# Token mixers of a hybrid block broken into parts and ordered by estimated ends of operations

## The chip, the cores and the metric

The kernel runs on one core of a Trainium2 chip. The metric is device time in microseconds (us). A profiled execution shows five engines: TensorE (PE; its weight loads are PEld), VectorE (DVE), ScalarE (ACT), GpSimd (POOL) and SyncE (SP), which starts most DMAs. An instruction stands in the queue of its engine and starts when the semaphores that it waits for have come.

## What is computed

Two layers of a hybrid backbone, batch 1, with 256 latent and 256 context tokens of width 1024. Four mixers read one input projection; their outputs are projected, gated and summed:

```
def token_mixers(hx, hc, p, rope_ret, rope_mla, need_ctx_out):
    (conv_x, z_x, xbc_x, dt_x, rq_x, rk_x, rv_x, rg_x, cq_x, ckv_x, kr_x, gl_x) = split_cols(hx @ p['w_in'], IN_SPLITS)
    ...
    ssm_yx, _ = ssm_mixer(z_x, xbc_x, dt_x, p, ssm_hc, True)
    ret_yx, _ = retention_mixer(rq_x, rk_x, rv_x, rg_x, p, ret_hc, rope_ret, True)
    att_x = block_attention(mla_q(cq_x, p, rope_mla), jnp.concatenate([k_c, k_x], axis=1), ...)
    out_x = merge_branches((conv_module(conv_x, p), ssm_yx, ret_yx, att_x), gl_x, p)
def conv_module(u, p):
    a, g = jnp.split(u, 2, axis=-1)
    h = dwconv(a * jax.nn.sigmoid(g), p['conv_w'], p['conv_b'])
    return jax.nn.silu(layernorm(h, p['conv_ln_g'], p['conv_ln_b']))
def merge_branches(branches, gate_logits, p):
    merged = sum(sigmoid(gate_i) * (branches[i] @ p['w_branch'][i]))
    return merged @ p['w_out']
```

(the last function is written shorter here). The convolution has 31 taps over 512 channels. Before the mixers stands a modulated RMS norm, behind them a SwiGLU block. In layer 1, the last, only the latent tokens are read on, so most of it works on N = 256 tokens, against N = 512 in layer 0.

## The kernel before

Activations lie transposed, channels on 128 partitions and tokens along the row. A float32 product is made of three fast matmuls of rounded halves (`mm3`): high by high, high by low, low by high. Weights come in one stream of chunks of 128 x 1024; for each, SP issues a 512 KB load (`raw`), ScalarE casts it (`whi`) and VectorE makes the remainder in two subtractions of 512 columns (`wlo`); `w_ensure` (line 347) keeps them some chunks ahead. Results of TensorE go to eight banks of 512 columns, four named `mm` (projections) and four named `mx` (mixers). All other tiles (`u`) come from 70 slots of a pool `U`.

The mixing stage of a layer is written by five generators. `lin` (line 740) holds what is TensorE's: the input projection (queries, keys, gated convolution inputs and so on), the gates, and the branch projections in the order state-space (1), MLA (3), retention (2), convolution (0); for branch i it waits for the token `br{i}`, which the mixer i gives. `ssm` (932), `ret` (1123), `mla` (1214) and `conv` (1344) are the mixers. Each `yield` gives the order back to `interleave` (585), and may name a token that must be there before the generator goes on, or, with a plus sign, give one. `interleave` takes `lin` by default, and a mixer when a count of VectorE's work (`clk["dve"]`, plain sums of durations, and `mixed`) lies more than LOOK behind the count of TensorE's. The mixers run in two rows, by MIX: `chain` (1384) runs ssm, mla and ret after one another, beside it stands `conv`. `conv` waits for `br1` and `br2` before its taps.

```
MIX = ("smr c", "smr c")
            w = min(can, key=lambda w_: steps[w_] if w_ else -1)
            if len(can) > 1 and w == 0 and max(clk["dve"], mixed) + lookahead < clk["pe"]:
                w = min(can[1:], key=lambda w_: steps[w_])
```

On TensorE the order of the program is kept for the mixers: `PE._place` ties each of their matmuls behind the last one of `lin` that was written before. On the other engines a scheduler goes by priorities: mostly the order of the program, with the work inside `tc.high_priority()` (weight preparation, evacuation of projections, row scales) ahead.

In `conv` a tap is one VectorE operation over a tile (`taps`, line 728); there are four tiles, in pairs. Then the four are added, `tok_sums` (502) sums the channels on TensorE (`mx<-one,u`), the mean is spread with `bcast` (532; `mx<-cons,mean`), subtracted, the squares are added, transposed and reduced (`rstd_of`, 513; `mx<-cons,u`), a row scale is made of ten tiny operations (`rs_y`), spread (`mx<-cons,rs_y`) and applied, followed by tanh and products. `tt` and `stt` are VectorE's two-operand helpers.

## Time and profile before

| | before |
|---|---|
| median of 3 runs | 1692.0 us (1687.25 to 1694.21) |
| profiled execution, its own time | 1692.55 us |
| its span, first to last instruction | 1690.8 us |
| mean granted TensorE clock | 0.994 |
| TensorE busy | 1641.8 us, 97% |
| VectorE busy | 1312.9 us, 78% |
| ScalarE busy | 812.0 us, 48% |

The mixers of layer 0 run mainly between 100 and 400 us of the span, those of layer 1 between 1100 and 1350; the last branch projection of layer 1 ends at about 1460. Busy time is the time in which an engine has an instruction at work; the share is that of the span. The ends of matmuls are modelled, so rows of TensorE overlap, and its pace is better read from start to start.

### The profile page before, as it was taken

What the parts mean: (1) busy time and instruction counts of PE and PEld (TensorE: products, weight loads), DVE (VectorE), ACT (ScalarE), POOL (GpSimd) and SP (SyncE); (2) the same over time, 40 slices, a digit from 0 to 9 for tenths busy, and PEclk for the clock granted to TensorE, in tenths of its full rate; (3) what the DMA queues carried; (4) which work ended last, traced back from release to release, by engine and by line L of the source; (5) the groups of instructions that cost most, each with busy time, mean ns of one, the idle gap of its engine ahead of it and who ended that gap; (6) DMA issues with size and microseconds to landing.
All of it is one profiled execution on the core that took longest, in us unless ns stands there. A gap on an engine that the chain in (4) does not pass through costs nothing.

```text
span 1690.8 us, 24270 instructions
## 1 busy us (share of the span) xinstructions
PE 1641.8 (97%) x8926; PEld 1359.7 (80%) x8926; DVE 1312.9 (78%) x2676; ACT 812.0 (48%) x1378; POOL 53.5 (3%) x89
## 2 busy tenths in 40 slices
PE   6999999999999999999999999999999999999998
PEld 4777766778888888988888889978778788778887
DVE  4779999988578568887666757699889967887765
ACT  3475759462234233522212235457577545455654
POOL 0020200000000000000000000001110000000000
PEclk9999999999999999999999999999999999999999
DMA  9353321214445445465456646445433377646664
GB/s 362 122 145 113 114 68 54 75 38 131 157 126 185 130 157 187 128 196 165 148 174 190 228 146 203 143 126 164 123 100 101 100 221 244 211 152 189 185 188 141
DMA packets 85096, 259.04 MB, mean 153 GB/s; under 512 B 9648, under 2 KB 18784, under 8 KB 84976
## 3 DMA queue, kind: packets, MB, share of 16 engines
q1 hardware_dynamic: 73584, 244.15, 45.8%
q10 hardware_dynamic: 10624, 12.28, 2.9%
q0 software_dynamic: 768, 1.05, 0.3%
q8 instruction: 70, 1.15, 0.3%
q14 instruction: 50, 0.41, 0.1%
HBM read 253.70 MB, written 2.18 MB: 151 GB/s over the span
## 4 chain that ended last, share of the span: by engine, by line
PE 86%; DVE 5%; DMA 4%; ACT 3%; issue 1%; POOL 0%; ACTq 0%; DVEq 0%; SPq 0%
PE mm L187 74%; PE mx L187 9%; DMA u<-drow 3%; PE mx L191 2%; DVE u L226 2%; ACT u L163 2%; DVE wlo L230 1%; DVE u L230 1%; ACT whi L168 1%; ACT u L168 1%; DVE u L241 0%; DMA u<-u 0%; DMA u<-xin 0%; DMA raw<-w_ada 0%; DMA drow<-u 0%
## 5 line engine op out<-in xcount | busy, mean ns | idle before, releaser
L187 PE MATMUL mm<-u,whi 128*128 128x512 f32 (+1 forms) x4088 | 1149.6, 362 | 3.7 <-DVE u L226 1.8
L187 PEld LDWEIGHTS mm<-u,whi 128*128 128x128 f32 x4088 | 728.1, 189 | 130.5 <-issue 12.1
L187 PE MATMUL mm<-u,wlo 128*128 128x256 f32 (+1 forms) x2332 | 785.3, 337 | 0.0
L168 ACT CAST whi<-raw 128x1024 fp32r<-128x1024 f32 x351 | 368.4, 1050 | 548.7 <-PE mm L187 328.8
L230 DVE TENSOR_TENSOR wlo<-raw,whi 128x512 fp32r<-128x512 f32 x702 | 461.7, 688 | 165.7 <-ACT whi L168 164.4
L187 PEld LDWEIGHTS mm<-u,wlo 128*128 128x128 f32 x2332 | 441.8, 189 | 47.0 <-issue 2.0
L226 DVE SCALAR_TENSOR_TENSOR u<-raw,cs,u 128x512 f32<-128x512 f32 x210 | 148.2, 746 | 80.7 <-DMA raw<-w_ada 80.6
L163 ACT ACTIVATE u<-u 128x256 f32<-128x256 f32 (+5 forms) x262 | 122.7, 484 | 150.5 <-DVE u L230 105.8
L187 PE MATMUL mm<-whi,u 128*128 128x512 f32 x544 | 172.7, 394 | 0.5 <-ACT u L163 0.5
L230 DVE TENSOR_TENSOR u<-u,u 128x256 f32<-128x256 f32 (+5 forms) x290 | 160.3, 571 | 8.3 <-ACT u L163 3.2
L187 PE MATMUL mx<-u,u 128*64 128x256 f32 (+6 forms) x644 | 132.1, 396 | 12.3 <-ACT whi L168 3.8
L226 DVE SCALAR_TENSOR_TENSOR u<-u,convw,u 128x510 f32<-128x510 f32 (+29 forms) x240 | 134.0, 599 | 0.0
L187 PEld LDWEIGHTS mx<-u,u 128*64 128x64 f32 (+3 forms) x644 | 79.8, 165 | 54.3 <-issue 13.5
L187 PEld LDWEIGHTS mm<-whi,u 128*128 128x128 f32 x544 | 101.8, 188 | 23.3 <-issue 1.7
L187 PE MATMUL mm<-wlo,u 128*128 128x512 f32 x272 | 106.4, 391 | 0.0
L163 ACT ACTIVATE u<-mm 128x512 f32<-128x512 f32 (+3 forms) x110 | 60.6, 553 | 40.1 <-PE mm L187 35.7
L226 DVE SCALAR_TENSOR_TENSOR u<-u,mm 128x512 f32<-128x512 f32 (+1 forms) x94 | 60.0, 647 | 19.8 <-PE mm L187 18.2
L226 DVE SCALAR_TENSOR_TENSOR u<-u,u 128x256 fp32r<-128x256 f32 (+3 forms) x113 | 61.0, 550 | 10.3 <-ACT u L163 10.3
L187 PEld LDWEIGHTS mm<-wlo,u 128*128 128x128 f32 x272 | 51.1, 188 | 10.7 <-issue 0.4
L168 ACT COPY u<-mx 128x512 f32<-128x512 f32 (+4 forms) x82 | 38.5, 495 | 38.1 <-PE mx L187 36.4
L191 PE MATMUL mx<-cons,u 128*128 128x128 f32 (+1 forms) x292 | 44.1, 276 | 4.8 <-DVE u L230 3.1
L1056 POOL TENSOR_SCALAR_AFFINE_SELECT u<-u 128x256 f32<-128x256 f32 x24 | 17.4, 726 | 983.2 <-DVE u L241 825.5
(116 smaller groups left out, 890.3 us busy)
## 6 DMA issues: line engine op xcount, KB each, us to landing
raw<-wst SPq DMA_DIRECT2D x354, 512.0 KB, 3.7
raw<-w_ada SPq DMA_DIRECT2D x72, 512.0 KB, 4.1
u<-wfirst SPq DMA_DIRECT2D x32, 256.0 KB, 6.0
u<-drow ACTq DMA_DIRECT2D x32, 256.0 KB, 4.7
u<-xin SPq DMA_DIRECT2D x16, 256.0 KB, 4.3
u<-w_ada SPq DMA_DIRECT2D x16, 256.0 KB, 5.3
u<-drow ACTq DMA_DIRECT2D x16, 128.0 KB, 3.9
spill<-u SPq DMA_DIRECT2D x8, 128.0 KB, 3.6
```

The costliest lines, as they stand in the source:

```text
L163: nc.scalar.activation(o, *a, **k)
L168: nc.scalar.copy(o, i)
L187: PE._place(nc.tensor.matmul(*a, **k))
L191: PE._place(nc.tensor.transpose(*a, **k))
L226: V.scalar_tensor_tensor(out=o, in0=i0, scalar=s, in1=i1, op0=op0, op1=op1)
L230: V.tensor_tensor(out=o, in0=i0, in1=i1, op=op)
L1056: G.affine_select(out=a_[:, 0:4:3], in_=a_[:, 0:4:3], pattern=[[0, 2], [1, 128]], compare_op=ALU.is_ge, fill=-1e5, base=0, channel_multipl ...
```

## The change

The mixers are cut into units, and their work is put in order by estimated times instead of sums. `spent` gives every operation an estimated end on its engine (`Line`, a timeline with gaps) and notes when its tile is ready (`done_at`) and when its inputs are free (`free_at`). A generator may then yield `at(...)`, an "@time": go on when TensorE's estimate has reached the time at which these tiles are ready. A token "#n" waits for n free slots of `U`. `stagger` runs up to two units of a row of mixers at once, if 12 slots are free. MIX has three rows now: ssm; mla and ret after one another; and conv, which is taken last. `interleave` takes the first mixer that can go on while VectorE's estimated work lies less than LEAD ahead of TensorE, then `lin`. `ret` and `mla` have units too (`turn`, `one_head`, `end`, and `setup` for mla), and the row scales are made by `rstd_later`, which yields between steps; so does `win`, once inside a projection. `conv` no longer waits for `br1` and `br2`, but for 18 free slots ahead of each pair of tiles, and its taps get a low priority. `urgent` is `tc.high_priority` together with a mark for the estimates. DMAs that GpSimd issues are not estimated.

```diff
-MIX = ("smr c", "smr c")
-LOOK = (7e3, 3e3)
-PACE = (1.4, 1.5)
+MIX = ("s mr c", "s mr c")
+LEAD = (6e3, 5e3)
...
+class Line:
+    def __init__(self):
+        self.t, self.gaps = 0.0, []
+    def ahead(self, now):
+        return self.t - now - sum(b - max(a, now) for a, b in self.gaps if b > now)
+    def put(self, ready, dur, now=0.0):
+        self.gaps = [g for g in self.gaps if g[1] > now]
+        for i, (a, b) in enumerate(self.gaps):
+            s = max(a, ready)
+            if s + dur <= b:
+                self.gaps[i:i + 1] = [g for g in ((a, s), (s + dur, b)) if g[1] - g[0] > 50]
+                return s + dur
+        s = max(self.t, ready)
+        if s - self.t > 50:
+            self.gaps.append((self.t, s))
+        self.t = s + dur
+        return self.t
...
+    def spent(e, o, ins, dur):
+        now = clk["pe"].t
+        r = max([done_at.get(i.tensor.name, 0.0) for i in ins if hasattr(i, "tensor")], default=0.0)
+        if e == "pe":
+            end = clk["pe"].t = max(now, r if who["now"] else 0.0) + dur
+        elif who["urgent"]:
+            end = max(now, r) + dur
+            clk[e].t = max(clk[e].t, now) + dur
+        else:
+            end = clk[e].put(max(r, now), dur, now)
+        done_at[o.tensor.name] = max(done_at.get(o.tensor.name, 0.0), end + (100 if e == "pe" else 130))
+        for i in ins:
+            if hasattr(i, "tensor"):
+                free_at[i.tensor.name] = max(free_at.get(i.tensor.name, 0.0), end)
+    def at(*ts_):
+        def last_(t):
+            return max(map(last_, t), default=0.0) if isinstance(t, (tuple, list)) else done_at.get(t.tensor.name, 0.0)
+        bank = free_at.get(banks[NMM - 8], 0.0) if len(banks) >= 8 - NMM else 0.0
+        return f"@{max(last_(ts_), bank) + 200}"
...
+        r = sm([128, len(sums), N // 128], "toks")
+        for i, tiles in enumerate(sums):
+            yield at(tiles)
+            p = mx()
+            for b in range(N // 128):
+                PE.transpose(p[:, b * 128:(b + 1) * 128], tiles[0][:, b * 128:(b + 1) * 128], ident)
+            red(r[:, i, :], p[:, :N].rearrange("p (b t) -> p b t", t=128), ADD)
+        ts(r, r, 1.0 / n, MUL, EPS, ADD)
+        rs = rsqrt(r, [128, len(sums), N // 128])
+        yield at(rs)
+        return rs
...
-    def interleave(lin, others, lookahead):
+    def met(r):
+        if r is None:
+            return True
+        if r[0] == "#":
+            return len(U.free) >= int(r[1:])
+        return float(r[1:]) <= clk["pe"].t if r[0] == "@" else r in who["done"]
+    def stagger(units, wide):
+        units, live = iter(units), []
+        while True:
+            n = next((n_ for n_, (_, r) in enumerate(live) if met(r)), None)
+            if n is None and len(live) < (wide if len(U.free) >= ROOM else 1):
+                g = next(units, None)
+                if g is not None:
+                    live.append((g, None))
+                    continue
+            if n is None:
+                if not live:
+                    return
+                late = [r for _, r in live if r[0] == "@"]
+                yield min(late, key=lambda r: float(r[1:])) if late else live[0][1]
+                if late or met(live[0][1]):
+                    n = next((n_ for n_, (_, r) in enumerate(live) if met(r)), None)
+                else:
+                    continue
+            g = live[n][0]
+            try:
+                r = next(g)
+            except StopIteration:
+                del live[n]
+                continue
+            if r is not None and r[0] == "+":
+                who["done"].add(r[1:])
+                r = None
+            live[n] = (g, r)
+            if r is None:
+                yield None
...
+    def interleave(lin, others):
         gens, done = [lin, *others], set()
-        mixed = clk["dve"]
-        alive, waits, steps = set(range(len(gens))), [None] * len(gens), [0] * len(gens)
+        who["done"] = done
+        alive, waits = set(range(len(gens))), [None] * len(gens)
+        def can(w):
+            return w in alive and met(waits[w])
         while alive:
-            can = [w for w in sorted(alive) if waits[w] is None or waits[w] in done]
-            assert can, waits
-            w = min(can, key=lambda w_: steps[w_] if w_ else -1)
-            if len(can) > 1 and w == 0 and max(clk["dve"], mixed) + lookahead < clk["pe"]:
-                w = min(can[1:], key=lambda w_: steps[w_])
+            ahead, few = clk["dve"].ahead(clk["pe"].t), len(U.free) < ROOM
+            conv = len(gens) - 1
+            w = next((w_ for w_ in range(1, conv + 1) if can(w_) and (ahead < LEAD[w_ == conv] or few and w_ < conv)), None)
+            if w is None and can(0) and not (few and any((waits[w_] or "-")[0] == "@" for w_ in alive)):
+                w = 0
+            if w is None:
+                w = next((w_ for w_ in range(1, len(gens)) if can(w_) and (w_ < conv or alive <= {0, conv})), None)
+            if w is None:
+                late = [(float(waits[w_][1:]), w_) for w_ in sorted(alive) if (waits[w_] or "-")[0] == "@"]
+                assert late, waits
+                w = min(late)[1]
             waits[w] = None
-            steps[w] += 1
-            before = clk["dve"], clk["act"]
             who["now"] = w
             try:
...
+            def end():
+                yield "squares0"
+                yield "squares1"
+                rs = yield from rstd_later(accs, N, 4 * 256)
+                U.put(accs)
+                for g in range(2):
+                    yield at(rs)
+                    rb = bcast(rs[:, g, :], N)
+                    for i in (2 * g, 2 * g + 1):
+                        stt(Y[i][:, :N], Y[i][:, :N], dpar[:, 4 + i:5 + i], rb[:, :N], MUL, MUL)
+                br[1] = [Y[i] for i in range(4)]
+                yield "+br1"
+            yield setup()
             for g in range(2):
-                rb = bcast(rs[:, g, :], N)
-                for i in (2 * g, 2 * g + 1):
-                    stt(Y[i][:, :N], Y[i][:, :N], dpar[:, 4 + i:5 + i], rb[:, :N], MUL, MUL)
-            br[1] = Y
-            yield "+br1"
+                u, xt, bc, gt = {}, {}, {}, []
+                for c in (2 * g, 2 * g + 1, 4 + g, 6 + g):
+                    yield short(c, xt, u, bc)
+                yield scores(g, bc, gt)
+                for pr in (2 * g, 2 * g + 1):
+                    yield two(pr, xt, u, gt)
+                yield squares(g, gt)
+            yield end()
...
+                kt, qt = kq.pop(h)
+                yield at(kt, qt)
+                px = first(kt, qt)
+                yield at(px)
+                pts[h] = second(px)
+                yield f"+weights{h}"
...
         def conv():
-            yield "br1"
-            hs = [U([128, N]) for _ in range(4)]
-            yield "br2"
+            hs = []
             for i in (0, 2):
                 yield f"gated{i + 1}"
+                yield "#18"
+                hs += [U([128, N]) for _ in range(2)]
                 gens = [taps(hs[i + e_], R["gated", i + e_], N,
                              lambda j, o=(i + e_) * CW: convw[:, o + j:o + j + 1], CW, P("convb", i + e_))
                         for e_ in range(2)]
-                for n_, _ in enumerate(zip(*gens)):
-                    if n_ % 2:
-                        yield
+                for n_ in range(CW + 1):
+                    with tc.high_priority(offset=-600):
+                        for g_ in gens:
+                            next(g_, None)
+                    yield
                 U.put(R.pop(("gated", i)), R.pop(("gated", i + 1)))
             t = U([128, N])
             tt(t[:, :N], hs[0][:, :N], hs[1][:, :N], ADD)
             for i in (2, 3):
                 tt(t[:, :N], t[:, :N], hs[i][:, :N], ADD)
+            yield at(t)
             m = sm([128, 1, nb], "mean")
             ts(m, tok_sums([[t]], N), 1.0 / 512, MUL)
             U.put(t)
+            yield at(m)
             mb = bcast(m[:, 0, :], N)
...
-        def chain(*gens):
-            for g in gens:
-                yield from g()
         parts = {"s": ssm, "m": mla, "r": ret, "c": conv}
-        clk["dve"] = clk["pe"] if last else began
-        interleave(lin(), [chain(*(parts[x] for x in w)) for w in MIX[l].split()], LOOK[l])
+        for e in ("dve", "act", "pool"):
+            clk[e].t, clk[e].gaps = clk["pe"].t, []
+        *ones, behind = MIX[l].split()
+        interleave(lin(), [stagger(itertools.chain(*(parts[x]() for x in y)), WIDE[l]) for y in ones] + [parts[behind]()])
```

The order of the instructions, of both versions, at three places of layer 1. In the names `mm` is a bank of a projection, `u_9403` and the like are the projections' inputs or mixer tiles, `whi` and `wlo` the weights.

TensorE around the convolution's normalization, before:

```order
L187 MATMUL mm_13365<-whi_13323,u_13103 128x512
L187 MATMUL mx_13413<-one,u_13408 128x1 [waits PE_49]
L187 MATMUL mx_13413<-one,u_13408 128x1
L187 MATMUL mm_13444<-whi_13368,u_9403 128x512 [waits Activation_49]
L187 MATMUL mm_13444<-wlo_13369,u_9403 128x512 [waits DVE_49]
L187 MATMUL mm_13444<-whi_13368,u_9404 128x512
L187 MATMUL mm_13445<-whi_13368,u_9403 128x512 [waits Activation_49]
L187 MATMUL mm_13445<-wlo_13369,u_9403 128x512
L187 MATMUL mm_13445<-whi_13368,u_9404 128x512
L191 MATMUL mx_13417<-cons,mean_13412 128x128 [waits DVE_49]
L191 MATMUL mx_13417<-cons,mean_13412 128x128
L187 MATMUL mm_13444<-whi_13368,u_9405 128x512
```

and in the changed kernel (`mm_13725` belongs to branch 2, `mm_13856` is the first projection of branch 0):

```order
L220 MATMUL mm_13725<-whi_13709,u_13677 128x512
L220 MATMUL mm_13725<-wlo_13710,u_13677 128x512
L220 MATMUL mm_13725<-whi_13709,u_13677 128x512
L220 MATMUL mx_13783<-one,u_13778 128x1 [waits DVE_49,PE_49]
L220 MATMUL mx_13783<-one,u_13778 128x1
L225 MATMUL mx_13787<-cons,mean_13782 128x128 [waits DVE_49]
L225 MATMUL mx_13787<-cons,mean_13782 128x128
L225 MATMUL mx_13804<-cons,u_13791 128x128 [waits DVE_49,PE_49]
L225 MATMUL mx_13804<-cons,u_13791 128x128
L225 MATMUL mx_13821<-cons,rs_y_13809 128x128 [waits DVE_49,PE_49]
L225 MATMUL mx_13821<-cons,rs_y_13809 128x128
L220 MATMUL mm_13856<-whi_13709,u_13844 128x512 [waits Activation_49]
```

Before, projections stood between the sums, the spread of the mean and the later steps; now these steps follow one another.

VectorE at the same place, before (the sums of the four tiles, `u_13408`, stand 50 rows further up, behind the last tap):

```order
L230 TENSOR_TENSOR wlo_13388<-raw_13302,whi_13387 128x512 [waits DMAHW3_49,Activation_49]
L230 TENSOR_TENSOR wlo_13388<-raw_13302,whi_13387 128x512
L226 SCALAR_TENSOR_TENSOR u_12868<-u_12868,mm_13364 128x512 [waits PE_49]
L226 SCALAR_TENSOR_TENSOR u_12870<-u_12870,mm_13365 128x512 [waits PE_49]
L239 TENSOR_SCALAR mean_13412<-mx_13413 128x2 [waits PE_49]
L230 TENSOR_TENSOR wlo_13449<-raw_13321,whi_13448 128x512 [waits DMAHW4_49,Activation_49]
L230 TENSOR_TENSOR wlo_13449<-raw_13321,whi_13448 128x512
L230 TENSOR_TENSOR u_11522<-u_11522,mx_13417 128x256 [waits PE_49]
L230 TENSOR_TENSOR u_11522<-u_11522,mx_13417 128x256
```

and in the changed kernel (in all 14 taps stand in a row from the ninth row on, then an addition to `u_13778`, two more taps and another addition; the mean comes next):

```order
L262 SCALAR_TENSOR_TENSOR u_13009<-u_11156,convw_9888,u_13009 128x244
L262 SCALAR_TENSOR_TENSOR u_13009<-u_11156,convw_9888,u_13009 128x245
L262 SCALAR_TENSOR_TENSOR u_13210<-u_13210,mm_13724 128x512 [waits PE_49]
L266 TENSOR_TENSOR wlo_13754<-raw_13688,whi_13753 128x512 [waits DMAHW0_49,Activation_49]
L262 SCALAR_TENSOR_TENSOR u_13212<-u_13212,mm_13725 128x512 [waits PE_49]
L266 TENSOR_TENSOR wlo_13754<-raw_13688,whi_13753 128x512
L266 TENSOR_TENSOR u_12355<-u_12355,u_13210 128x512 [waits DVE_49]
L266 TENSOR_TENSOR u_12357<-u_12357,u_13212 128x512 [waits DVE_49]
L262 SCALAR_TENSOR_TENSOR u_13009<-u_11156,convw_9888,u_13009 128x244
L262 SCALAR_TENSOR_TENSOR u_13009<-u_11156,convw_9888,u_13009 128x245
```

The taps of the second pair of tiles now stand last, behind the additions for branch 2.

TensorE at the first output of the state-space mixer, before:

```order
L187 MATMUL mm_11488<-u_9404,whi_11299 128x512
L187 MATMUL mm_11488<-u_9403,wlo_11300 128x512
L187 MATMUL mm_11488<-u_9405,whi_11299 128x512
L187 MATMUL mm_11488<-u_9406,whi_11299 128x512
L187 MATMUL mx_11438<-u_11347,u_10690 64x256 [waits DVE_49,Activation_49]
L191 MATMUL mx_11456<-cons,u_10619 128x128 x2
L187 MATMUL mm_11488<-u_9405,wlo_11300 128x512
L187 MATMUL mm_11488<-u_9407,whi_11299 128x512
```

and in the changed kernel:

```order
L220 MATMUL mm_11159<-u_9403,wlo_11096 128x256 [waits DVE_49]
L220 MATMUL mm_11159<-u_9405,whi_11095 128x256
L225 MATMUL mx_10760<-cons,rs_y_10748 128x128 [waits DVE_49,PE_49]
L225 MATMUL mx_10760<-cons,rs_y_10748 128x128 x3
L220 MATMUL mx_10881<-u_10546,u_10393 64x256 [waits PE_49]
L220 MATMUL mx_10881<-u_10578,u_10393 64x256
```

The output's matmuls (`64x256`) waited for VectorE and ScalarE; now they follow the spreads of a row scale and wait for TensorE's own banks alone.

## Rows read from the trace of the kernel before

**Rows 1.** The page's part 1: engine, busy us, share of the span, instructions.

```profile
PE 1641.8 (97%) x8926; PEld 1359.7 (80%) x8926; DVE 1312.9 (78%) x2676; ACT 812.0 (48%) x1378; POOL 53.5 (3%) x89
```

**Rows 2.** Windows: busy us of PE, PEld, DVE, ACT, POOL; clock; DMA share.

```profile
100.00:400.00 300.00, 291.76 (x1397) 219.72 (x1396) 282.78 (x571) 191.53 (x386) 26.36 (x38) 0.99 0.29 86
1100.00:1350.00 250.00, 239.67 (x1368) 197.27 (x1367) 227.92 (x553) 162.82 (x319) 25.59 (x40) 0.98 0.41 119
1343.00:1462.00 119.00, 117.55 (x528) 96.48 (x526) 89.98 (x175) 60.44 (x80) 0.00 (x0) 1.00 0.73 234
1419.00:1455.00 36.00, 36.00 (x161) 29.59 (x160) 31.81 (x58) 19.47 (x27) 0.00 (x0) 1.00 0.83 276
```

**Rows 3.** The same for instructions that read the convolution's weights, VectorE alone.

```profile
62.00:412.00 350.00, 84.76 (x124) 1.00 0.31 92
1343.00:1462.00 119.00, 4.06 (x10) 1.00 0.73 234
```

**Rows 4.** What TensorE waited for, 100 to 400: us in total, times, longest.

```profile
PE mx L191 <- DVE rs_y L226: 2.1, 3, 1.7
PE mx L187 <- ACT u L163: 2.0, 2, 1.6
```

**Rows 5.** The same, 1110 to 1350.

```profile
PE mx L187 <- ACT whi L168: 3.8, 1, 3.8
PE mx L187 <- DVE u L226: 1.9, 1, 1.9
PE mx L187 <- DMA u<-u: 1.9, 1, 1.9
```

**Rows 6.** TensorE's timeline: start, us, operation, xcount [idle before <-releaser].

```profile
1203.76 1.08 PE L187 MATMUL mx<-u,u 128*64 128x256 f32 x2 [3.83 <-ACT whi L168]
...
1205.69 1.05 PE L187 MATMUL mm<-u,whi 128*128 128x512 f32 x2
...
1206.97 1.05 PE L187 MATMUL mm<-u,whi 128*128 128x512 f32 x2
...
1209.47 0.63 PE L187 MATMUL mm<-u,whi 128*128 128x512 f32 x2
```

**Rows 7.** Windows (columns as above) around short stops.

```profile
240.00:250.00 10.00, 7.54 (x24) 4.23 (x25) 8.94 (x19) 9.75 (x27) 0.00 (x0) 0.84 0.01 2
1205.00:1210.00 5.00, 5.00 (x15) 4.00 (x15) 3.94 (x11) 1.03 (x3) 1.74 (x1) 0.56 0.33 105
1230.00:1240.00 10.00, 7.80 (x40) 6.42 (x39) 6.86 (x12) 6.66 (x15) 5.00 (x10) 0.84 0.80 166
```

**Rows 8.** VectorE's timeline, normalization of the convolution in layer 1.

```profile
1402.23 1.28 DVE L226 SCALAR_TENSOR_TENSOR u<-u,mm 128x512 f32<-128x512 f32 x2
1403.43 0.15 DVE L239 TENSOR_SCALAR mean<-mx 128x2 f32<-128x2 f32 x1
...
1404.95 1.41 DVE L230 TENSOR_TENSOR u<-u,mx 128x256 f32<-128x256 f32 x4
...
1414.48 0.43 DVE L234 TENSOR_REDUCE toks<-mx 128x2 f32<-128x256 f32 x1 [0.52 <-PE mx L191]
...
1417.83 0.16 DVE L226 SCALAR_TENSOR_TENSOR rs_y<-rs_s,rs_y 128x2 f32<-128x2 f32 x1
```

**Rows 9.** VectorE's timeline beside the stop of rows 6.

```profile
1208.13 0.43 DVE L230 TENSOR_TENSOR u<-u,u 128x256 f32<-128x256 f32 x1 [1.05 <-ACT u L163]
...
1209.41 0.41 DVE L241 TENSOR_SCALAR u<-u,convw,par 128x256 f32<-128x256 f32 x1
1209.73 1.66 DVE L226 SCALAR_TENSOR_TENSOR u<-u,convw,u 128x255 f32<-128x255 f32 x4
```

**Rows 10.** ScalarE's timeline, the squares of that normalization.

```profile
1407.07 1.03 ACT L163 ACTIVATE u<-u 128x256 f32<-128x256 f32 x3
```

**Rows 11.** TensorE's timeline, transposes and spread of that normalization.

```profile
1414.06 0.38 PE L191 MATMUL mx<-cons,u 128*128 128x128 f32 x2
...
1418.13 0.40 PE L191 MATMUL mx<-cons,rs_y 128*128 128x128 f32 x2 [0.27 <-DVE rs_y L226]
```

More of the change, by code (lines that the diff above doesn't have):

```diff
@@ L530, in rstd_of, with rstd_later @@
         return rsqrt(r, shape)
+    def rstd_later(sums, N, n):
+        r = sm([128, len(sums), N // 128], "toks")
+        for tiles in sums:
+            if len(tiles) == 2:
+                t = tiles.pop()
+                tt(tiles[0][:, :N], tiles[0][:, :N], t[:, :N], ADD)
+                U.put(t)
+        for i, tiles in enumerate(sums):
[8 more added lines that the diff above has]
+        return rs
     def bcast(r, N):
@@ L771, in lin @@
                 for i in range(nt):
[L772 removed]
+                    ps = yield from win(name, i, n)
                     t = U([128, n])
[L774 removed]
+                    with urgent():
                         A.copy(t[:, :n], ps[:, :n])
@@ L957, in ssm @@
-            p = mx()
-            for i, mname in enumerate(("triu", "tril", "ones")):
-                PE.matmul(p[:, 64 * i:64 * i + 64], C(mname), la.rearrange("p b h -> p (b h)"), start=True, stop=True,
-                          skip_group_check=True)
-            A.copy(cum, p[:, 0:192].rearrange("p (i b h) -> p i b h", i=3, b=4))
-            lc, std, nlc, st = (sm([128, 4, 16], n_, bufs=1) for n_ in ("lc", "std", "nlc", "st"))
-            ld = sm([128, 4, 16], "ld", bufs=1)
-            ts(ld, dt, 1e-37, MAX)
@@ new lines, in short @@
+            def short(c, xt, u, bc):
+                yield f"xbc{c}"
+                n = N if c >= 6 else T
+                y, t = U([128, n]), U([128, n])
+                for _ in taps(y, R["xbc", c], n, lambda j: P("scw", c * 5 + j), 5, P("scb", c)):
+                    pass
+                U.put(R.pop(("xbc", c)))
+                A.activation(t[:, :n], y[:, :n], AF.Tanh, scale=0.5)
+                stt(y[:, :n], t[:, :n], 1.0, y[:, :n], ADD, MUL)
+                U.put(t)
+                if c < 4:
+                    u[c] = y
+                    yield at(y)
+                    p = mx()
+                    for b in range(4):
+                        PE.transpose(p[:, b * 128:(b + 1) * 128], y[:, b * 128:(b + 1) * 128], ident)
+                    xt[c] = operand(True, p, [128, 512], 0.5)[0]
+                else:
+                    bc[c] = operand(fs, y, [128, n])
+                yield f"+short{c}"
@@ L1022, in ssm, with scores @@
+            def scores(g, bc, gt):
+                yield f"short{4 + g}"
+                yield f"short{6 + g}"
+                bo, co = bc.pop(4 + g), bc.pop(6 + g)
                 for kst, qst in ((0, 0), (1, 0), (1, 1))[:1 + ns]:
+                    yield at(bo, co)
                     p = mx()
```

511 lines of the change are left out of this document (276 added, 235 removed).

## The prediction, made before the changed kernel ran

> **What bounds the kernel now.** I read the share of each engine first, then the stretches, then what ended TensorE's waits, then single instructions. TensorE is busy 1641.8 of 1690.8 us, VectorE 1312.9 [rows 1]. The change moves no arithmetic: the order of both versions holds the same matmuls, and beside them one more 512 KB weight chunk (a cast and two subtractions). So only TensorE's idle time and its clock can change, and only where the mixers run. The stretches [rows 2] say how much is there. Between 100 and 400 us (mixers of layer 0) TensorE is busy 291.76 of 300, so 8.24 idle; between 1100 and 1350 (layer 1) 239.67 of 250, so 10.33 idle. VectorE is nearly full in both (282.78 and 227.92): they are limited by both engines, alternately. From 1343 to 1462, where only gates and branch projections are left, TensorE is full (117.55 of 119) and VectorE is busy 89.98, so it has 29 to spare. The long convolution lies the other way round [rows 3]: 84.76 us of VectorE (124 taps) between 62 and 412, and 10 operations in the projections of layer 1. The change moves taps from the crowded stretches to the spare one; its worth is what it takes off the waits, less what the late taps cost.
>
> **What can be gained.** In layer 0 the waits are short and scattered; the longest are 1.7 us for a row scale (rs_y) and 1.6 us for a ScalarE result [rows 4]. Two mixer streams let the other's matmuls stand in such a wait, and 39 of the 124 taps leave VectorE's queue ahead of the last softmax (87 stood there, now 48). Bounds: 0 if the waits are only exchanged, 8.24 if all go. I take 6, nearer the upper end, since each wait named there is for a result that now stands behind other matmuls. In layer 1 three waits make most of the 10.33: 3.8, 1.9 and 1.9 us [rows 5]. The first is that of the state-space output (mx<-u,u 64x256): before, it carries waits for VectorE and ScalarE, now it follows four spreads of a row scale that VectorE computes later than its operands, and waits for TensorE's own work alone. The DMA of the third brings the keys' rotated rows. In exchange the new order has, where retention's keys are turned, seven small matmuls close together with waits on VectorE. Bounds 0 and 10.33; I take 8, nearer the upper end, because the longest wait is certain to go.
>
> The clock is the third gain. After the 3.83-us stop at 1203.76 three matmuls of 512 columns are started every 1.28 us (1205.69 to 1206.97) [rows 6], and in the projections 161 take 36.00, so three take 0.67 [rows 2]: half speed. The granted clock from 1205 to 1210 is 0.56 [rows 7], which is the lower of the two levels (1.2 GHz) for most of it: some 2.2 us lost. At 1230 to 1240 it is 0.84, in layer 0 at 240 to 250 also 0.84, so 10 us at 0.84 each cost up to 1.6. I take 3 for layer 1 and 1 for layer 0, with 0 and 5.4 as bounds. Gains: 6 + 8 + 3 + 1 = **18 us**, bounds 0 and 24.
>
> **What is added.** *The end of the long convolution in layer 1.* Before, its four sums were long ready, and its normalization ran under the projections: between sums, mean, squares and row scale the order holds 6, 42 and 15 projection matmuls, and 161 stand behind [rows 2]. Now the second pair of tiles waits for 18 free slots, and its taps end VectorE's work: in the order shown with the change, TensorE's column sums (mx<-one,u) stand behind the last independent matmul, and nothing but the chain itself follows up to the first projection of branch 0. Step by step:
> - VectorE still has, from the last wait for a projection on, six operations of 512 columns, a pair of which takes 1.20 us (1402.23 to 1403.43) [rows 8]: 3.6. Then 16 taps and two additions of 256 columns; four taps take 1.66 [rows 9], so 18 x 0.41 = 7.4. The first of the six waits for the last tile but one of the projections, and everything after it stands behind that wait. Together 11.0, of which some 0.7 lie beside TensorE's last three matmuls: 10.3.
> - VectorE may be late already. From the last retention scores on, TensorE has some 217 matmuls of 0.224, eight of retention in full float32 (an estimate of 0.4 each, less than twice that price) and a few transposes, about 54 us; VectorE's order up to the same point holds 43 taps (17.6), 34 subtractions of 512 columns (20.4), 31 others (15) and ten tiny ones (2), 55. So they are level, and each wait of VectorE goes straight through: between 0 and 6, I take 1.7.
> - The normalization stands bare: sums 0.4, mean 0.15 [rows 8], spread 0.38, four subtractions 1.41, squares 1.03 (three) [rows 10], additions 0.9, transposes 0.38 [rows 11], reduction 0.43, the row scale until 1417.99 less a pair of weight subtractions 1.8, spread 0.40 and a wait of 0.27; then scale, tanh, shift, product and cast of the first tile, five passes of about 0.45 [rows 8]: 2.3. That is 9.9; handing over between engines adds, tiles that overlap take off, TensorE's own 1.6 is no idle time. I take 9.5, bounds 8 and 12.
> - Such a stop is longer than the one at 1203.76, so the clock falls: 2.2 as at [rows 6], 0 to 3.
> Sum: 10.3 + 1.7 + 9.5 + 2.2 = **23.7 us**, bounds 18 and 31.
>
> In layer 0 the normalization keeps projections around it (30 matmuls between its steps), so nothing is added. The weight work was covered by the 29 us that VectorE has to spare in the projections; in the last 50 us of them that cover is gone, which the second step counts. The extra chunk: ScalarE, VectorE and DMA have room at its place, 0, at most one pair, 1.3. The DMAs of the keys' rotated rows in layer 1 go through GpSimd and are not in the planner's estimates; the 1.9-us wait for one [rows 5] may stay. That is why I left 2.3 of the 10.33 in.
>
> A filler at low priority is only that in the order that is written down. When the program ran, VectorE waited 1.05 us for ScalarE ahead of 1208.13 while the convolution's first operation of a tile, at 1209.41, with all its operands long there, stood behind [rows 9]; no tap filled the hole. The Trainium skill ("TensorE: Matmul & The Clock Gate", the opening table, row on engine queue depth) calls VectorE's queue strictly first in, first out, and this trace agrees; if taps could be taken early instead, the 7.4 us of the first step would go, and the lateness with them, and the sum would be 1689.
>
> **The sum.** -18 + 23.7 = +5.7 on the profiled execution's 1692.55: 1698.2, forecast **1698**. That execution lies 0.5 us above the median of the runs, 1692.0, so nothing is corrected. Half a per cent of that, 8.5 us, is about what a measurement can tell from no change: faster is below 1683.5, slower above 1700.5.
>
> **Rivals.**
> *A, the forecast's case:* gains of 14 to 22 and an end of 20 to 27 give 1690 to 1706. For it: order and prices above. Chance 0.55, of which 0.42 same and 0.13 slower.
> *B, slower:* VectorE is late at the end of layer 1. If its queue from the retention on loses more than 4 us to waits (a late cast, a late score), each is a wait for weights, and the end costs 26 to 31, while only half the gains come (9 to 13): 1706 to 1715, middle 1710. For it: VectorE is level with TensorE there. Against: the stretch is 54 us long and TensorE can run one chunk ahead. It decides from about 26 us of end. Chance 0.22, all slower.
> *C, faster:* all waits go and the end is short. Interleaving works in full: 8.24 + 10.33 + 5.4 less the bare end of 12 (VectorE ahead by the time of the last taps, the chain without a gap): 1680. For it: idle time and VectorE's spare 29 us. Against: taps stand last in VectorE's order in any case. Chance 0.12, of which 0.09 faster. The Trainium skill ("Perfetto Trace Analysis", Optimization Strategy) holds that a kernel whose most contended engine changes over time may gain by interleaving those regimes; that is what would happen here, and [rows 2] show two such regimes, but the taps are put behind the second, not into it.
> *D, nothing:* the estimates order the work as short of waits as before, and the end overlaps with VectorE's idle time: both terms below 5, 1692. Against: the order around the convolution's end is changed beyond doubt. Chance 0.11, 0.10 same and 0.01 slower.
>
> Faster 0.09, same 0.55, slower 0.36. The range 1684 to 1711 leaves out C's lower part (about 0.09) and B's upper half (about 0.11).
>
> **What would show it.** Right: in layer 1 TensorE idles some 20 us in one place, before the first projection of branch 0, broken only by sums, transposes and spreads; VectorE is full of taps ahead of it; the clock is low after it; the 3.8-us wait is gone, and 100 to 400 idles 2 to 3 us. The first step is wrong if the sums start within 5 us of the last independent matmul, the gains if idle time up to the projections is above 12 in all. The forecast is wrong altogether if the end is below 12 us or time appears outside the mixers.

## The result and the profile after

| | before | changed |
|---|---|---|
| median | 1689.79 us (8 runs) | 1699.65 us (8 runs) |
| ratio, 95% interval | 1 | 1.0065 (1.0048 to 1.0081) |
| lowest to highest | 1687.25 to 1694.21 | 1697.39 to 1708.41 |
| profiled execution, its own time | 1692.55 us | 1708.41 us |
| mean granted TensorE clock in it | 0.994 | 0.984 |

The change made the kernel slower by 0.65%, some 11 us; a loss of 5.7 had been forecast, and 1699.65 lies inside the stated range of 1684 to 1711. The profiled execution of the changed kernel is its slowest of eight, so its parts are a few us too long in sum; the experiments below repeat the comparison from medians.

The page's part 1 of the changed kernel answers to [rows 1]: the same work, TensorE and VectorE busy as before.

```profile
PE 1637.9 (96%) x8926; PEld 1363.0 (80%) x8926; DVE 1320.0 (77%) x2678; ACT 812.0 (48%) x1379; POOL 50.7 (3%) x89
```

Three marks that stand in both programs cut the span into parts: the column sums of the second norm of layer 0 (the mixing stage of layer 0 is over), of the first norm of layer 1, and of the second norm of layer 1. TensorE's timeline (start, duration, operation, count) before:

```profile
673.14 0.35 PE L187 MATMUL mx<-one,u 128*128 128x1 f32 x2
...
1071.93 0.28 PE L187 MATMUL mx<-one,u 128*128 128x1 f32 x2
...
1485.39 0.38 PE L187 MATMUL mx<-one,u 128*128 128x1 f32 x2
```

and in the changed kernel:

```profile
664.04 0.35 PE L220 MATMUL mx<-one,u 128*128 128x1 f32 x2
...
1062.71 0.28 PE L220 MATMUL mx<-one,u 128*128 128x1 f32 x2
...
1497.54 0.38 PE L220 MATMUL mx<-one,u 128*128 128x1 f32 x2 [2.11 <-DVE u L266]
```

Up to the first mark the changed kernel is 9.1 us faster. Between the first and the second both take 399. From the second to the third, the mixing stage of layer 1, it takes 434.8 against 413.5: 21.4 slower. What TensorE waited for in that stage (1060 to 1480; us in total, times, longest), the first four lines:

```profile
PE mx L220 <- DVE u L266: 10.9, 2, 10.5
PE mx L225 <- DVE u L266: 9.0, 3, 3.7
PE mx L225 <- DVE rs_y L262: 5.7, 3, 2.8
PE mm L220 <- ACT u L194: 4.2, 1, 4.2
```

The 3.8 us of [rows 5] is gone, and so are the two of 1.9; in their place stand longer ones. Most of them lie in one spot. TensorE's timeline there:

```profile
1429.83 0.39 PE L220 MATMUL mm<-whi,u 128*128 128x512 f32 x1
1440.74 0.99 PE L220 MATMUL mx<-one,u 128*128 128x1 f32 x4 [10.53 <-DVE u L266]
1441.98 0.69 PE L225 MATMUL mx<-cons,mean 128*128 128x128 f32 x2 [0.25 <-DVE mean L275]
1445.66 0.66 PE L225 MATMUL mx<-cons,u 128*128 128x128 f32 x2 [2.99 <-DVE u L266]
1448.92 0.66 PE L225 MATMUL mx<-cons,rs_y 128*128 128x128 f32 x2 [2.59 <-DVE rs_y L262]
1453.79 0.80 PE L220 MATMUL mm<-whi,u 128*128 128x512 f32 x1 [4.21 <-ACT u L194]
```

The last independent projection ends at 1430.2, the first one of branch 0 starts at 1453.8, and between them stand the convolution's sums, mean, squares and row scale with nothing else. The five stops add up to 10.53 + 0.25 + 2.99 + 2.59 + 4.21 = 20.6 us. VectorE's timeline beside the first of them:

```profile
1432.28 1.28 DVE L266 TENSOR_TENSOR u<-u,u 128x512 f32<-128x512 f32 x2
1433.49 5.43 DVE L262 SCALAR_TENSOR_TENSOR u<-u,convw,u 128x244 f32<-128x244 f32 x14
1438.84 0.41 DVE L266 TENSOR_TENSOR u<-u,u 128x256 f32<-128x256 f32 x1
1439.17 0.96 DVE L262 SCALAR_TENSOR_TENSOR u<-u,convw,u 128x241 f32<-128x241 f32 x2
1440.17 0.42 DVE L266 TENSOR_TENSOR u<-u,u 128x256 f32<-128x256 f32 x1
```

After the last two additions for branch 2 it works through 16 taps and two additions, 7.1 us in a row; the sums start when they end.

The clock fell three times here. Windows of the changed kernel (columns as in [rows 2]):

```profile
1440.00:1454.00 14.00, 3.21 (x11) 2.01 (x12) 8.80 (x30) 5.28 (x15) 0.00 (x0) 0.50 0.02 6
1454.00:1460.00 6.00, 6.00 (x20) 4.83 (x21) 2.52 (x6) 1.95 (x5) 0.00 (x0) 0.74 0.00 0
1470.00:1475.00 5.00, 4.90 (x21) 4.15 (x21) 2.75 (x8) 2.10 (x6) 0.00 (x0) 0.66 0.28 105
1498.00:1505.00 7.00, 7.00 (x56) 3.72 (x58) 1.62 (x10) 0.00 (x0) 0.00 (x0) 0.51 0.22 68
```

At a clock of 0.50, the lower of the two levels, TensorE does in a busy microsecond about half of what it does at 1.00 (three matmuls of 512 columns in 1.28 us against 0.67, [rows 6, 2]). Busy time by what is missing to 1.00 gives 3.21 x 0.50 + 6.00 x 0.26 + 4.90 x 0.34 = 4.8 us up to the third mark, and 7.00 x 0.49 = 3.4 us behind it, 8.3 us in all. Behind the third mark the changed kernel needs 209.2 us to its last instruction, the kernel before 205.4.

Idle time up to the end of the mixers changed little. Windows before:

```profile
100.00:450.00 350.00, 341.76 (x1618) 261.10 (x1617) 315.17 (x620) 204.28 (x401) 26.36 (x38) 1.00 0.32 96
1100.00:1400.00 300.00, 289.67 (x1589) 238.66 (x1588) 259.10 (x609) 186.31 (x346) 25.59 (x40) 0.98 0.46 135
```

and in the changed kernel:

```profile
100.00:450.00 350.00, 341.84 (x1660) 266.17 (x1659) 322.35 (x633) 206.01 (x404) 24.19 (x39) 1.00 0.33 101
1100.00:1400.00 300.00, 291.01 (x1602) 243.74 (x1601) 243.70 (x559) 188.15 (x344) 25.07 (x40) 0.98 0.47 140
100.00:400.00 300.00, 293.11 (x1440) 225.96 (x1439) 275.34 (x558) 193.25 (x388) 24.19 (x39) 0.99 0.31 91
1100.00:1350.00 250.00, 241.41 (x1368) 204.84 (x1367) 198.36 (x451) 156.96 (x291) 20.43 (x32) 0.97 0.48 142
```

TensorE is idle for 8.24 us of the first stretch before and for 8.16 after, for 10.3 and 9.0 of the second. In the shorter stretches of the prediction (100 to 400, 1100 to 1350) 8.24 and 10.33 [rows 2] became 6.9 and 8.6. But TensorE gets through more: 1660 matmuls against 1618 in the first stretch. Where that comes from is seen in the group of the mixers' own matmuls (up to 664 us, all of layer 0's in both; busy us and mean ns behind the bar), before:

```profile
L187 PE MATMUL mx<-u,u 128*64 128x256 f32 (+6 forms) x388 | 78.0, 393 | 3.8 <-ACT u L163 2.0 <-ACT u L168 0.9 <-DVE u L230 0.9
```

and in the changed kernel:

```profile
L220 PE MATMUL mx<-u,u 128*64 128x256 f32 (+6 forms) x388 | 71.5, 388 | 3.5 <-DVE u L266 3.4
```

The same 388 matmuls are busy for 6.5 us less. Neighbours overlap in such a busy time, so it is better to count from each start to the next start on TensorE, less the idle time that the trace lists. By that count, up to the first mark, these 388 take 67.5 us against 73.0, all matmuls into the mixers' banks (`mx`) 122.4 against 129.7, those into the projections' banks (`mm`) 517.8 against 518.0, and the listed idle time is 11.0 against 12.4. So 7.3 of the 9.1 us lie in the pace of the mixers' matmuls. Short waits can hide there: a matmul of 512 columns is drawn 0.39 us long where the next one starts 0.22 us behind it (1428.24 and 1428.46 in the changed kernel), and a wait shorter than the rest makes no idle time. That the 7.3 us are such waits is likely but not shown.

### The profile page after: what moved, and what is told of

Read it like the earlier page. It is cut to its first block, busy times and chain, and to the rows that moved or that the text cites. A ratio compares the mean times of both kernels' runs of the same rounds, so it can differ in the third digit from the quotient of the medians.

```text
span 1706.7 us, 24303 instructions
## 1 busy us (share of the span) xinstructions
PE 1637.9 (96%) x8926; PEld 1363.0 (80%) x8926; DVE 1320.0 (77%) x2678; ACT 812.0 (48%) x1379; POOL 50.7 (3%) x89
## 4 chain that ended last, share of the span: by engine, by line
PE 77%; DVE 6%; issue 1%; ACT 1%; DMA 1%; POOL 0%; ACTq 0%; DVEq 0%; POOLq 0%
PE mm L220 68%; PE mx L220 7%; DVE u L262 2%; PE mx L225 2%; DVE wlo L266 2%; DVE u L266 1%; ACT whi L199 1%; DMA u<-drow 1%; ACT u L194 1%; POOL u L345 0%; DVE u L277 0%; ACT u L199 0%; ACTq L189 0%; DVE vmean L270 0%; DVE rs_s L266 0%
## 5 line engine op out<-in xcount | busy, mean ns | idle before, releaser
L220 PEld LDWEIGHTS mm<-u,whi 128*128 128x128 f32 x4088 | 729.3, 190 | 128.1 <-issue 10.2
L220 PE MATMUL mm<-u,wlo 128*128 128x512 f32 (+1 forms) x2332 | 786.2, 337 | 1.1 <-DVE wlo L266 1.1
L194 ACT ACTIVATE u<-u 128x256 f32<-128x256 f32 (+6 forms) x262 | 122.3, 484 | 160.2 <-DVE u L266 119.7
L266 DVE TENSOR_TENSOR u<-u,u 128x512 f32<-128x512 f32 (+6 forms) x288 | 159.7, 572 | 14.1 <-ACT u L194 6.9
L262 DVE SCALAR_TENSOR_TENSOR u<-u,convw,u 128x510 f32<-128x510 f32 (+28 forms) x240 | 132.6, 601 | 0.1
L220 PE MATMUL mx<-u,u 128*64 128x256 f32 (+5 forms) x644 | 118.1, 389 | 4.0 <-DVE u L266 3.4
L220 PEld LDWEIGHTS mx<-u,u 128*64 128x64 f32 (+3 forms) x644 | 76.3, 163 | 39.9 <-issue 12.5
L345 POOL TENSOR_SCALAR_AFFINE_SELECT u<-u 128x256 f32<-128x256 f32 (+1 forms) x64 | 42.0, 657 | 1206.4 <-DVE u L277 980.2
L262 DVE SCALAR_TENSOR_TENSOR u<-u,u 128x256 f32<-128x256 f32 (+3 forms) x112 | 61.1, 553 | 17.7 <-ACT u L194 17.7
L220 PEld LDWEIGHTS mm<-wlo,u 128*128 128x128 f32 x272 | 51.6, 190 | 10.2
L199 ACT COPY u<-mm 128x256 f32<-128x256 f32 (+2 forms) x98 | 45.3, 465 | 25.0 <-PE mm L220 18.5
```

The costliest lines, as they stand in the source:

```text
L194: nc.scalar.activation(o, i, *a, **k)
L199: nc.scalar.copy(o, i)
L220: PE._place(nc.tensor.matmul(o, a, b, **k))
L262: V.scalar_tensor_tensor(out=o, in0=i0, scalar=s, in1=i1, op0=op0, op1=op1)
L266: V.tensor_tensor(out=o, in0=i0, in1=i1, op=op)
L345: G.affine_select(out=out, in_=in_, **k)
```

## Experiments

All are edits of the changed kernel. The ratio is to the kernel before, timed on the same chip. The last two columns are from the one profiled execution of each: the time up to the end of layer 0's mixing stage (the first mark) and the length from the second mark to the third.

| run | edit | median us | ratio (95%) | first mark | layer 1 |
|---|---|---|---|---|---|
| before | | 1689.8 | 1 | 673.1 | 413.5 |
| change | | 1699.7 | 1.0065 (1.0048 to 1.0081) | 664.0 | 434.8 |
| e0 | none, one execution | 1708.1 | | 666.0 | 432.9 |
| e8 | none, timed again | 1704.4 | 1.0068 (1.0047 to 1.0089) | 669.8 | 430.7 |
| e1 | 10 slots in layer 1 | 1694.9 | 1.0016 (0.9993 to 1.0039) | 665.3 | 424.3 |
| e2 | taps at ordinary priority | 1706.8 | 1.0099 (1.0075 to 1.0123) | 663.2 | 431.8 |
| e3 | e1, one row in layer 1 | 1674.5 | 0.9902 (0.9878 to 0.9926) | 669.9 | 402.9 |
| e4 | one row in layer 1 alone | 1705.5 | 1.0087 (1.0058 to 1.0115) | 666.2 | 431.7 |
| e5 | e1, 7 us of lead | 1676.5 | 0.9910 (0.9884 to 0.9936) | 664.8 | 403.2 |
| e6 | e3, one row in layer 0 too | 1694.1 | 1.0012 (0.9999 to 1.0026) | 686.7 | 402.9 |
| e7 | e3, 1200 ns of patience | 1681.5 | 0.9939 (0.9915 to 0.9963) | 656.0 | 417.4 |
| e9 | 7 us of lead alone | 1709.1 | 1.0076 (1.0047 to 1.0106) | 669.7 | 433.4 |
| e10 | e5, patience in layer 0 | 1672.8 | 0.9864 (0.9839 to 0.9888) | 661.8 | 404.9 |

The first mark of programs with the same layer 0 (all but before, e2, e6, e7 and e10) lies between 664.0 and 669.9: what happens ahead of layer 1 varies by some 6 us from one execution to the next.

**e0 and e8: the change again.** No edit.

> The changed kernel once more, unaltered, for a second profile. Theory A (the end of the long convolution in layer 1 costs some 20 us bare, order alone decides it): the stop before the column sums is 10 to 11 us again, the four later stops together 9.5 to 10.5, the span 1696 to 1703. Theory B (the 8.7 us by which the first profiled execution lies above the median come from the stops of the mixing stage, so that those vary from run to run): the stops of this profile are shorter by several us in all.

The five stops were 10.54, 0.25, 2.99, 2.58 and 4.21, within 0.01 of the first profile: they belong to the order. No stop was shorter by more than 0.01, so B falls by its own test. The span was 1706.4, above A's 1696 to 1703. The three profiled executions of this order (1708.4, 1708.1 and 1710.6 with e8) all lie above the medians of 1699.7 and 1704.4. Their granted clocks, 0.984, 0.982 and 0.983, are among the lowest of the 17 executions of this order (0.981 to 0.990); where else the excess lies is not shown.

> The changed kernel unaltered, timed on the same chip as the two kernels beside it. Theory A: 1697 to 1708, with the 10.5-us stop and 9.5 to 10.5 us of stops in the chain again.

1704.36 at a ratio of 1.0068, as at first. Stops again 10.54, 0.25, 2.99, 2.59 and 4.21.

**e1: the second pair of tiles starts earlier.**

```diff
-                yield "#18"
+                yield "#18" if not last else "#10"
```

> In layer 1 the convolution's pairs of tiles wait for 10 free slots instead of 18; nothing else is changed. Theory A (the second pair starts too late, so that VectorE is left with its taps when the projections run out): the 10.5-us stop before the column sums goes, the mean's part is covered, the row scale (2.6) and the products and cast after it (4.2) stay bare; 13 to 17 us faster than the changed kernel, 1683 to 1687. Rival B (VectorE is full in any case between the retention and the end, so the taps only move the wait to the weights): the stop goes but waits for weight remainders take its place, 1695 to 1700.

1694.9: 8 us faster by the ratios (1.0016 against 1.0065), not 13 to 17. The stop before the sums is gone, and no wait for weights has come in its place, so B falls. But more of the chain stays bare than was expected. TensorE's timeline at its end:

```profile
1423.77 0.96 PE L220 MATMUL mm<-whi,u 128*128 128x512 f32 x3 [2.14 <-DVE u L262]
...
1440.54 0.66 PE L225 MATMUL mx<-cons,rs_y 128*128 128x128 f32 x2 [5.55 <-DVE rs_y L262]
1445.41 0.80 PE L220 MATMUL mm<-whi,u 128*128 128x512 f32 x1 [4.21 <-ACT u L194]
```

The squares' transposes and the spread of the row scale still stand behind the last projection, because the planner takes a step of the convolution only while its estimate for VectorE lies less than 5 us ahead (e5 changes that). Reduction and row scale wait as one (5.55), and the product of the first tile for branch 2 is now late as well (2.14).

**e2: ordinary priority for the taps.**

```diff
-                    with tc.high_priority(offset=-600):
+                    if True:
```

> The taps have the ordinary priority of their place in the program; the 18 slots stay. Theory A (late start, not low priority): the second pair starts as late as before, VectorE has the same work left, the idle time before the column sums shrinks by up to 7 but waits for weights and mixers grow by nearly as much: 1696 to 1701. Rival B (low priority puts the taps last and costs the 7.4 us of them): 1690 to 1693.

1706.8, above both ranges and no faster than the change (the edit acts on both layers). The stop before the sums shrinks to 6.63, but another for VectorE grows ahead of it, and the chain is bare as before:

```profile
1420.12 1.65 PE L220 MATMUL mm<-whi,u 128*128 128x512 f32 x3 [2.72 <-DVE u L262]
...
1437.45 0.98 PE L220 MATMUL mx<-one,u 128*128 128x1 f32 x4 [6.63 <-DVE u L266]
```

Layer 1 takes 431.8, as in the change (430.7 to 434.8). So the low priority is not the cause: with a late start VectorE has the same work left, wherever it stands.

**e4 and e3: one row of mixers in layer 1, with the bare end and without it.** e4 is the first line, e3 has e1's edit too.

```diff
-MIX = ("s mr c", "s mr c")
+MIX = ("s mr c", "smr c")
```

> In layer 1 the three mixers run in one row (ssm, mla, ret), as in e3, but the convolution waits for 18 free slots, as in the change; its sums then stand behind the last independent projection again. Theory A (only whether the end of the convolution is covered counts in layer 1): as slow as the changed kernel, 1696 to 1706, with a stop of some 10 us before the sums and 9 to 10 in the chain. Rival B (the second row of mixers in layer 1 is itself what costs, so that e3 owes its gain to the single row): within 6 us of e3's 1674.5.

> As e1_gate10, and in layer 1 the three mixers run in one row again (ssm, mla, ret after one another, still in units and by estimated ends). Theory A (in layer 1 running MLA beside the state-space mixer bought nothing, the stops were only exchanged): within 4 us of e1_gate10. Rival B (the second row covers waits in layer 1): 6 to 12 us slower than e1_gate10.

e4: 1705.5, as A had it; TensorE waits 13.1 us before the sums, then for the same four stops as in the change, 10.0 us together. e3: 1674.5, twenty below e1, which neither theory had. With one row the convolution is planned earlier: ahead of its sums TensorE has 7360 of its 8926 matmuls, not 7440 as in e1 (7568 in the change), the whole chain stands ahead of other branches' projections, and no stop of it is left. Its layer 1 takes 402.9; of its mixers' stops the longest is that of the change (3.7), the one for the row scale is shorter (1.2 against 2.8). The single row by itself gives nothing (e4 against e8: 1.0087 against 1.0068); what it gave in e3 was the cover.

**e5: two rows, the end covered.** e1's edit, and in `interleave` (a part of one line is shown):

```diff
-(ahead < LEAD[w_ == conv] or few and w_ < conv)
+(ahead < (7e3 if l and w_ == conv else LEAD[w_ == conv]) or few and w_ < conv)
```

> Two rows of mixers in layer 1 as in the change, 10 slots, and the convolution may be taken in layer 1 while VectorE's estimate lies up to 7 us ahead, not 5. Its sums then stand some 340 TensorE rows ahead of the last projection, the chain is covered. Theory A (the bare end is the whole loss): no stop in the chain, 1672 to 1679, like e3. Rival B (two rows cost in layer 1 whatever the end does): 1686 to 1694.

1676.5, in A's range. From 1030 to 1460, TensorE waited for these and nothing else:

```profile
PE mx L225 <- DVE u L266: 6.0, 3, 3.7
PE mx L225 <- DVE rs_y L262: 2.2, 1, 2.2
PE mx L220 <- DVE u L266: 0.4, 1, 0.4
```

Its mixers' stretch of layer 1:

```profile
1100.00:1400.00 300.00, 293.05 (x1623) 243.39 (x1622) 263.57 (x628) 195.20 (x360) 24.83 (x40) 0.99 0.48 145
```

TensorE idles 6.95 us there, against 10.33 before the change. Layer 1 takes 403.2, 10.2 less than before the change, and 27.5 to 31.6 less than in the three profiles of the change. By the ratios the end cost 1.0068 - 0.9910, 1.6% or 27 us (by the two intervals some 6 either way), and without it the change would gain 0.9%, 15 us.

**e9: the lead without the slots.** e5's second edit alone.

> As the change (two rows, 18 slots), and in layer 1 the convolution may be taken while VectorE's estimate lies up to 7 us ahead, not 5: e5 without its 10 slots. In the order the sums then stand some 58 TensorE rows ahead of the end of the independent projections, the chain's last two steps at the end. Theory A (each step of the chain that lies bare costs its stop, and the late taps theirs): the 10.5 us before the sums go or turn into a shorter wait, 7 to 10 of the chain stay; 1685 to 1692, between the change and e5. Rival B (the slots alone decide, the lead does nothing): 1697 to 1708.

Neither: 1709.1, just above B's range, but not for B's reason. The lead did move the sums forward, from 7568 matmuls ahead of them to 7512. Now they and the retention's row scale collide. VectorE's timeline just before the sums:

```profile
1428.52 0.47 DVE L262 SCALAR_TENSOR_TENSOR u<-u,convw,u 128x242 f32<-128x242 f32 x1
1428.91 0.16 DVE L262 SCALAR_TENSOR_TENSOR rs_s<-rs_s 128x8 f32<-128x8 f32 x1
1429.03 0.47 DVE L262 SCALAR_TENSOR_TENSOR u<-u,convw,u 128x242 f32<-128x242 f32 x1
1429.42 0.16 DVE L262 SCALAR_TENSOR_TENSOR rs_y<-rs_s,rs_y 128x8 f32<-128x8 f32 x1
```

and TensorE's:

```profile
1431.12 0.98 PE L220 MATMUL mx<-one,u 128*128 128x1 f32 x4 [8.56 <-DVE rs_y L262]
...
1455.52 0.66 PE L225 MATMUL mx<-cons,rs_y 128*128 128x128 f32 x2 [4.75 <-DVE rs_y L262]
1460.44 0.79 PE L220 MATMUL mm<-whi,u 128*128 128x512 f32 x1 [4.26 <-ACT u L194]
```

A tap stands between any two steps of the row scale, so that each step takes 0.51 us instead of some 0.20 (as in the same run from 1454.24 to 1455.21, where the steps follow one another). The slots are what lets the taps start early enough; the lead places the chain once they are done.

**e6: one row in layer 0 too.** On e3:

```diff
-MIX = ("s mr c", "smr c")
+MIX = ("smr c", "smr c")
```

> As e3, and in layer 0 too the mixers run in one row. Theory A (the gain of 7 to 9 us in layer 0 comes from MLA beside the state-space mixer): it is lost, 1680 to 1685. Rival B (it comes from the units and the estimated ends, the rows do not matter): 1672 to 1677.

1694.1: 19.6 us slower than e3, more than A had, and its layer 1 is the same (402.9). Its first mark lies at 686.7. In layer 0 the second row is worth more than the whole change gains there: cut into units and ordered by estimated ends, but in one row, layer 0 is 13.5 us behind the kernel before.

**e7: more patience everywhere**, on e3, and **e10: in layer 0 alone**, on e5. The second is the first with `200 if l else 1200`.

```diff
-        return f"@{max(last_(ts_), bank) + 200}"
+        return f"@{max(last_(ts_), bank) + 1200}"
```

> As e3, and every wait for an estimated end asks for 1200 ns more instead of 200. Theory A (the stops that are left in the mixing stage, 3.7, 3.4 and 1.2 us, are for tiles that come a microsecond or two later than estimated): they shrink by half, 1668 to 1673. Rival B (the lateness is VectorE's queue as a whole, and more patience only moves work): 1673 to 1680.

> e5 (two rows, 10 slots and 7 us of lead in layer 1), and in layer 0 alone 1200 ns of patience behind every estimated end, which in e7 made layer 0 shorter by some 10 us and layer 1 longer by 14. Theory A (the layers are independent of each other): 1664 to 1670. Rival B (layer 0's gain in e7 came from its chip run alone; layer 0 varies by 7 us between runs of the same order): 1672 to 1679.

e7: 1681.5, above both ranges. Layer 0 ended at 656.0, earlier than in any other run, layer 1 took 14 us longer than in e3; it has a new stop of 5.7 us before the convolution's sums, which now have 7186 matmuls ahead of them. So patience costs time in layer 1, and may help in layer 0. e10 tries it there alone: ratio 0.9864 against e5's 0.9910, 7.8 us, on different chips, and it beats both kernels: 1.4% below the kernel before, and 1672.8 us against the change's 1704.4 on the same chip. But 1672.8 lies in B's range and not in A's, the intervals of e5 and e10 touch, the spans of their profiles are 1672.5 and 1671.2, and the first mark (661.8 against e5's 664.8) moved by less than it varies between executions of one order. Whether patience helps layer 0 stays open.

## Why the prediction was right, and where it was off

**Direction and range: right.** 1698 was forecast, 1699.65 measured; the ratio puts the loss at 11 us against 5.7. The forecast called the result within 0.5% with 0.55 and slower with 0.36; the measured 0.65% lies just past that edge.

**The first step, VectorE's last work: right.** 10.3 for the stop before the sums; 10.53 measured, with the same 16 taps and two additions (7.1 instead of 7.4). The sums did not start within 5 us of the last projection.

**VectorE's lateness: not there.** 1.7 was added; the stop leaves 0.2 for it. Rival B with it: VectorE kept up, and the gains did not halve.

**The bare chain: right.** 9.5 forecast; 0.25 + 2.99 + 2.59 + 4.21 = 10.0.

**The clock after it: too small, and the step that failed most.** 2.2 was taken from the one stop of [rows 6], with 0 and 3 as bounds. Not one stop stands there but three groups: the chain, 2.31 us at 1469.88 and 2.11 at 1497.54, each with the lower clock behind it, 8.3 us by the windows above. The 2.11 is a stop that the kernel before did not have at that place either, and the sum had no term for it. e0, e1, e2 and e8 have the same two stops. e4 and e9, whose ends are bare too, have neither (0.93 and 1.30 us, and 0.89 and 1.31, at the first place, none at the third mark), so they come with some orders and not with every bare end. Up to the third mark 20.6 + 4.8 + 2.1 = 27.5 us, where layer 1 of the three profiles is 27.5 to 31.6 longer than in e5; the rest is not assigned. With the 3.4 behind the mark it is 31.0 in this profile, and some 27 by the ratios of e5 and e8, which go by medians. 23.7 had been forecast, 18 to 31 as bounds.

**The gains: right in sum, wrong in place.** 18 were forecast, 15 came (e5 against the kernel before). Layer 0: 7 forecast; 9.1 in the first profile, 6.5 as the mean of three, against the one profile of the kernel before. Layer 1: 11 forecast, 10.2 in e5. By the prediction's own sign the step is wrong all the same: idle time up to the projections was to be at most 12 in all, and it is 6.9 + 8.6 = 15.5. The prediction took the gains from the idle time listed in [rows 2, 4, 5], and most of them did not lie there: up to the end of the mixers 8.24 idle became 8.16, and 10.3 became 9.0 (6.95 in e5, where that is 3.4 of the 10.2). Listed waits were mostly exchanged for others of the same size, as the bound "0 if the waits are only exchanged" had it; a 3.8-us stop went and a 3.7-us stop came. In layer 0 the gain lies in the mixers' own matmuls, 129.7 us against 122.4 from start to start, which the trace does not show as idle. The clause that 100 to 400 would idle for 2 to 3 us is refuted: 6.9. That the term came out at nearly the right size was luck. The weight loads do show that TensorE got through more: in the same 350 us they are busy 261.10 before and 266.17 after, while TensorE's matmuls are busy 341.8 in both. The Trainium skill ("Perfetto Trace Analysis", Identifying the Most-Contended Engine) holds that busy time of matmuls is no good measure of how near a kernel is to its limit, because they are pipelined, and has the busy time of weight loads, with the share of peak arithmetic, used instead; these two windows agree.

**Rivals.** e5 comes near C's time, 1676.5 against 1680, but not as C had it: C let all listed waits go and left an end of 12 us, while in e5 no stop of the end is left and TensorE still idles 6.95 us from 1100 to 1400. The Trainium skill's sentence on interleaving regimes ("Perfetto Trace Analysis", Optimization Strategy) is borne out by e5 and e10, 0.9 and 1.4% faster than before, and by the change itself only up to the end of the mixers. That a filler of low priority is one only in the written order is borne out by e9, where the taps stand between the steps of a row scale and each step waits for one; e2 shows only that another order of the same work gave about the same time.

**Open.** Why the gain in the mixers' own matmuls is as large as it is was not tried further. Why the first mark varies by 6 us between executions of one order is seen in part: from 446 to 460 us the granted clock is 0.76 in e8 and 0.88 in e3 and e9, the three latest (669.7 to 669.9), and 1.00 in the other five (664.0 to 666.2). Why the clock fell there in some executions and not in others is not shown.

## What to carry to other kernels

Filler work is free only while something independent is left to run beside it *and beside everything that hangs on it*: look in the written order for the place where the last independent matmul of the stage stands, and count what VectorE still has to do and how many hand-overs follow. A filler that starts by free buffers starts late exactly where buffers are scarce; moving its start (10 slots for 18) together with the place of its tail was worth 27 us here, either alone 8 or nothing, and its priority nothing. Idle time in the trace is no upper bound for what a better order can gain: compare too what the same group of instructions takes from start to start.

## What the runs showed of the hardware that was not expected

Stops of 2.31 and 2.11 us, after some 14 and 26 us of work that itself followed a longer stop, were each followed by TensorE's lower clock (0.66 from 1470 to 1475, 0.51 from 1498 to 1505); before the change, two stops of 0.94 and 1.31 us at the first of these places left it at 1.00 (1460 to 1465). Not every stop of such a length did it: after 2.79 us, ahead of 1188.26 in the changed kernel, the clock was low (0.66 from 1186 to 1196), after 2.77 us, ahead of 1185.41 in e2, it was not (1.00 over the same window); and in e9 stops of 0.89 and 1.31 us at the first place were followed by the lower level (0.57 from 1478 to 1482). What decides is not shown here. Once the clock was down in the chain, it stayed down through four short pieces of work (0.50 from 1440 to 1454) and 3.3 us of full work behind them, until about 1457.1 (0.50 from 1456 to 1457, 0.94 from 1457 to 1458).
